# FFN parts of 6, 8 and 8 pairs in place of 8, 7 and 7, with fourteen pairs per FFN as seven block products

## The chip, the cores and the metric

The kernel runs on one core of a Trainium2 chip. The metric is the device time of one execution in microseconds (us), as the median of several; lower is better. All products are made in single precision by splitting each float32 operand into a high and a low part (names that end in hi and lo) and adding three matmuls: high by high, high by low, low by high.

## The reference

A trunk of two layers works on 512 tokens of width 1024 with 16 learned tokens put ahead of them, 528 columns in all. A layer is a mixer (attention, a convolution module and a short convolution side by side) and a feed-forward network (FFN). The change concerns the FFN, and the first step of the next mixer:

```python
def ffn_sublayer(h, pre_g, post_g, w_up, conv_w, w_down):
    u = rms_norm(h, pre_g)
    z = jnp.einsum("bld,df->blf", u, w_up)
    z = causal_depthwise_conv(z, conv_w)
    g, up = jnp.split(z, 2, axis=-1)
    y = jnp.einsum("blf,fd->bld", jax.nn.silu(g) * up, w_down)
    return h + rms_norm(y, post_g)

def reference(x, meta_tokens, ...):
    ...
    for l in range(DEPTH):
        h = mixer_sublayer(h, ...)
        h = ffn_sublayer(h, ...)
    return h[:, N_META:]
```

The hidden width of the FFN is 2816, so w_up makes 2 x 2816 columns: a gate half and an up half.

## The kernel before, in words

**Pairs and parts.** The hidden width is cut into 22 chunks of 128. A *pair* f is the gate chunk and the up chunk with that number. The FFN runs in parts of pairs (PARTS, L29). A part makes the up products of its pairs one after the other, sends each pair through the convolution and the gate (ffn_gate, around L2171 to L2191), which gives one g tile per pair (a high and a low part, the tiles y), and then makes the *down* products of the part: for each of eight output blocks m, the sum over the part's g tiles. Parts 0 and 1 add into the tile yp on the way (L2412: a copy by ScalarE in part 0, a sum by VectorE in part 1); the last part is merged with the normalisation that follows and with the next mixer's first products (finish, L2435). In the last layer the down of parts 0 and 1 is 512 wide and that of the last part is in two halves of 256.

**Whole pairs.** A whole pair is two chunks of 8 blocks of the inner dimension, three matmuls each, in two halves of the columns: 96 matmuls (mm3, L837).

**Pairs as seven block products.** For pairs in SEVEN, seven_pair (L2293) treats the gate and up chunks, and the two halves of the inner dimension, as a 2 x 2 block matrix, and the two column halves of the inputs likewise, and makes seven block products of 12 matmuls in place of eight: 84 matmuls (product, L2288). Its inputs are four sums of blocks of u, the tiles t0 to t3, made once per FFN by normalised (L2212), whose steps are handed out by build between other work. Its weights are the gate chunk itself and three more parts called c, b and d: c and b are read from sums of weight blocks (w_sum in DRAM), d is half of the up chunk. prep_one (L616) loads each part, splits it (ACT casts the high part, L641; DVE subtracts to get the low part, L642), and puts it into tiles: c into the rotating whi and wlo, d into the tile of the largest part's last g, and b into shi and slo, of which there is **one each**.

**The sums of weights** are made ahead, in DRAM, at five kinds of places, which SUMS lists per layer: place 0, in the FFN of the layer before; place 1, in the layer's mixer (L1846: SP copies blocks, and POOL adds with accumulating DMAs; sum_steps, put at L534); place 2, in the FFN by tick (after each g tile one step behind a POOL copy, L2206); places 3 and 4, in the down of parts 0 and 1, by loads to the chip, sums on VectorE and stores (down_sum, L575). Sums are taken in the order of the pairs that need them.

**Stored splits.** While layer 0 runs, six chunks of the next mixer's input weights are split and written to DRAM (w_split), so that the next mixer can load the two parts without splitting. store_one (L663) does one step: it takes the chunk that the call before fetched, casts it into shi on ACT (L666), subtracts into slo on DVE (L667), has POOL write both to DRAM (L670), and fetches the next chunk. It uses the same shi and slo as part b of a seven-product pair. Seven calls do all six: the first only fetches, the last only stores. AHEAD_SPLITS (L2349) lists the pairs of layer 0 ahead of which they stand: two each before pairs 8, 9 and 10 and one before 11.

**What sets the order.** The FFN's up products and the downs of parts 0 and 1 are given in program order and put in order by a scheduler, engine by engine; every engine runs its own instructions strictly in that order and waits on what others have to deliver. issue_after keeps an instruction from standing ahead of a named one on its engine. PE is TensorE, DVE VectorE, ACT ScalarE, POOL GpSimd and SP the engine that issues most loads.

Of the kernel before, what the change touches and what calls it, by code (L numbers as in the profile page):

```python
# [18 lines left out]
KD = D // P  # L19
# [6 lines left out]
CK = 31  # L26
DFF = 2816
NF = DFF // P
PARTS = (8, 7, 7)  # L29


SUMS = (((), (11, 12, 13), (15, 16), (17, 18), (19, 20)),
        ((8, 9), (10, 11, 12, 13), (15, 16), (17, 18), (19, 20)))
SEVEN = tuple(sorted(sum(places, ())) for places in SUMS)
NEXT_SUMS, AHEAD_SPLITS = 13, (8, 8, 9, 9, 10, 10, 11)
SUM_US, SUM_LAT, SUM_EVERY = 0.9, 9.0, 40.0
K2 = KD // 2
SB = K2 * P
AHEAD = 2
# [350 lines left out]
def tile_hybrid_trunk(ctx: ExitStack, tc: tile.TileContext, xT, wflat, pv_d, out):  # L390
# [158 lines left out]
    def sums_at(l, place):  # L549

        return SUMS[l][place] if l < DEPTH else ()

# [572 lines left out]
    def mixer(l, ypool, first, close_first, spans, front, rzs, u_at):  # L1125
# [719 lines left out]

        for i, f in enumerate(sums_at(l, 1)):  # L1846
            copies, *adds = sum_steps(l, f)
            tok = flow.op("sp", 2.0, copies, (Tok(flow.pe + SUM_EVERY * i),), prio=8, lat=SUM_LAT)
            for op in adds:
                tok = gp(SUM_US, op, tok, prio=8, lat=SUM_LAT)  # L1850

# [168 lines left out]
    def y_pair(i):  # L2020
        t = T(ypool, [P, 2, L], F32R, f"y{i}")
        return t[:, 0], t[:, 1]
# [71 lines left out]
    for l in range(DEPTH):  # L2094
# [23 lines left out]
        with tc.tile_pool(name=f"fp{l}", bufs=2, reuse_waits="tile") as fp:  # L2118
# [91 lines left out]
            def normalised():  # L2210
# [39 lines left out]
                        yield lambda b=b, k=k: un(b, k)  # L2250
                for k in range(0, K2, 2):
                    if k:
                        yield None
                        yield lambda: block(0)
                        yield None
                    yield lambda: total(2, k, lambda: at(b12), lambda: at(b22))
                    yield lambda: split(2, k)
                    yield lambda: total(0, k, lambda: at(b11), lambda: at(b12))
                    yield lambda: total(1, k, lambda: at(b22), lambda: raw[0], ALU.add)
                    yield lambda: split(0, k)  # L2260
                    yield lambda: total(3, k, lambda: at(b21), lambda: raw[1])
                    yield lambda: split(1, k)
                    yield lambda: split(3, k)
# [4 lines left out]

            mul_ins, glo_ins, ghi_ins = [None], [None], {}
            ts, n_seven, primed = [], [0], set()  # L2270
            building = [None]

            def build(n):

# [70 lines left out]
            for part, nf in enumerate(PARTS):  # L2345
                for f in range(f0, f0 + nf):
                    if g:
                        tick(g[max(g)][0][:, :1])
                    for _ in range(AHEAD_SPLITS.count(f) if l == 0 else 0):  # L2349
                        store_one()  # L2350
                    if f in seven:
                        seven_pair(f)
                        if f == seven[-1]:
# [29 lines left out]
                if seven and part == 0:  # L2383
                    for k in range(0, KD, 4):
                        nc.sync.dma_start(h_dram[:, k:k + 4], h[:, k:k + 4])
                    spare[0] = h
                if part < len(PARTS) - 1:
                    more = down_sums(l, part)
                    for op in more.pop(-1):
                        op()  # L2390
                    for some in ((0, 1), *((m,) for m in range(2, KD))):
# [12 lines left out]
                        for m, ps in zip(some, tiles):  # L2404
# [8 lines left out]
                            for op in more.pop(m, ()):  # L2413
                                with tc.issue_after(evac.ins), tc.issue_after(last_low[0].ins):
                                    op()
                else:
                    assert not todo and not later and building[0] is None
                    if seven:
# [3 lines left out]
                    gpre = None if final else pvs[l + 1][1][:, _COLS["mix_pre_g"]:]  # L2422
                    first = raw = rzs = None
                    if not final:
                        raw = list(zip(*[g[f0 + k] for k in range(nf)], y_pair(nf)))
                        raw = [[[t[:, half_sl(hf)] for t in ts] for ts in raw] if hf < 2 else None for hf in range(2)]
                        rzs = [rz[:, half_sl(hf)] if raw[hf] else None for hf in range(2)]
                        first = First(lambda b, k, hf, raw=raw: raw[hf][b][k] if raw[hf] else u_rhs(b, k, hf), [H, H], {})
# [62 lines left out]
```

## Time and profile before

| | |
|---|---|
| median of the runs before | 1264.08 us (1263.58 to 1264.17) |
| the profiled execution | 1262.1 us, span of the core 1260.4 us |
| mean granted TensorE clock | 0.999 |
| whole pairs of layer 0's FFN, part 0 | within 276.5 to 411 us |
| seven-product pairs of layer 0, last part | within 518.3 to 568 us |
| seven-product pairs of layer 1, last part | within 1134 to 1183 us |

In the rows of the profile, "psum<-t,whi" names the output and the inputs of an instruction by the program's names; 128x264 is its tile, "x1107" a number of instructions. A bracket "[0.35 <-ACT zs L2373]" means that the engine stood idle for 0.35 us ahead of that instruction, until ACT's instruction on zs at line 2373 let it go. Matmul records overlap, so what one matmul costs is the spacing of the starts, not the printed length. "uhi, ulo" are the split input of a product, "t" the sums of blocks of it. Where a weight is loaded to the tile h or raw, it is the same kind of load into another free place.

### The profile page before, as it was taken

The numbers are of one execution on the slowest core, as the hardware profiler recorded it, in microseconds if no ns is written. First come the engines' busy times: TensorE is split into PE (matmuls) and PEld (weight loads), VectorE is DVE, ScalarE is ACT, GpSimd is POOL, SyncE is SP. The second block draws the span as 40 slices with busy tenths as digits, with TensorE's granted clock in tenths as the row PEclk, the third lists the DMA queues.
The fourth block names the chain that finished last, engine by engine and source line by source line (L and its number), as shares of the span: only waits on it lengthen the run. The fifth ranks groups of instructions, "written<-read, shape, count | busy, mean of one in ns | idle before, by whom it ended". The sixth has DMA issues, their size and how long they took to land.

```text
span 1260.4 us, 24292 instructions
## 1 busy us (share of the span) xinstructions
PE 1244.2 (99%) x9554; PEld 1194.4 (95%) x9554; DVE 926.0 (73%) x1581; ACT 710.3 (56%) x1377; POOL 175.9 (14%) x360
## 2 busy tenths in 40 slices
PE   8999999999999999999999999999999999999997
PEld 8999898999999999999999988999999899989997
DVE  7887866589874776487688877756799748757954
ACT  7254576655444663476673545775554447526763
POOL 1323411001111001010003244110022000000000
PEclk9999999999999999999999999999999999999999
DMA  7267551726658755765652684547166565465611
GB/s 245 80 154 180 122 118 47 256 88 150 185 146 339 243 192 153 243 193 169 209 186 68 157 194 109 144 116 238 70 166 177 148 212 172 151 228 178 203 60 67
DMA packets 80755, 206.59 MB, mean 164 GB/s; under 512 B 8624, under 2 KB 18992, under 8 KB 80128
## 3 DMA queue, kind: packets, MB, share of 16 engines
q1 hardware_dynamic: 66976, 168.20, 42.1%
q0 software_dynamic: 13664, 36.84, 13.0%
q8 instruction: 75, 1.23, 0.4%
q14 instruction: 40, 0.33, 0.1%
HBM read 170.82 MB, written 50.60 MB: 176 GB/s over the span
## 4 chain that ended last, share of the span: by engine, by line
PE 94%; DVE 2%; ACT 1%; DMA 1%; POOL 1%; issue 0%; SPq 0%; DVEq 0%; ACTq 0%
PE psum L837 63%; PE psum L2288 17%; PE psum L1407 5%; PE psum L1671 3%; PE psum L1637 2%; PE psum L974 1%; PE psum L1593 1%; PE psum L1737 1%; PE psum L1323 1%; DMA raw<-in_w_dram 0%; POOL dm L1608 0%; DMA h<-in_x_dram 0%; DVE yp L1050 0%; DVE h L1060 0%; PE psum L1617 0%
## 5 line engine op out<-in xcount | busy, mean ns | idle before, releaser
L837 PE MATMUL psum<-y,whi 128*128 128x264 f32 (+3 forms) x1968 | 383.8, 299 | 0.8 <-DVE zs L989 0.7
L837 PEld LDWEIGHTS psum<-y,whi 128*128 128x128 f32 x1968 | 305.8, 188 | 13.7 <-DVE zs L989 0.9
L837 PE MATMUL psum<-uhi,whi 128*128 128x264 f32 (+1 forms) x1168 | 292.2, 289 | 1.5 <-ACT uhi L2069 0.8
L837 PE MATMUL psum<-ulo,whi 128*128 128x264 f32 (+1 forms) x1168 | 286.0, 284 | 0.6 <-DVE ulo L2071 0.4
L837 PE MATMUL psum<-uhi,wlo 128*128 128x264 f32 (+1 forms) x1168 | 285.3, 284 | 0.0
L837 PE MATMUL psum<-y,wlo 128*128 128x264 f32 (+3 forms) x984 | 274.0, 297 | 0.7 <-DVE wlo L793 0.7
L837 PEld LDWEIGHTS psum<-uhi,whi 128*128 128x128 f32 x1168 | 201.7, 189 | 5.9 <-issue 1.6
L837 PEld LDWEIGHTS psum<-ulo,whi 128*128 128x128 f32 x1168 | 201.8, 189 | 1.3 <-DVE ulo L2071 0.6
L837 PEld LDWEIGHTS psum<-uhi,wlo 128*128 128x128 f32 x1168 | 201.5, 189 | 0.0
L837 PEld LDWEIGHTS psum<-y,wlo 128*128 128x128 f32 x984 | 178.0, 188 | 6.4 <-DVE wlo L793 1.1
L2173 DVE SCALAR_TENSOR_TENSOR c<-zs,pv,c 128x528 f32<-128x528 f32 (+1 forms) x176 | 130.5, 756 | 21.2 <-ACT c L2171 19.9
L652 ACT CAST whi<-raw 128x1024 fp32r<-128x1024 f32 (+1 forms) x65 | 66.1, 1021 | 96.9 <-PE psum L837 74.3
L793 DVE TENSOR_TENSOR wlo<-raw,whi 128x1024 fp32r<-128x1024 f32 (+2 forms) x80 | 95.6, 1204 | 31.1 <-ACT whi L789 30.5
L789 ACT CAST whi<-raw 128x1024 fp32r<-128x1024 f32 (+2 forms) x80 | 81.7, 1030 | 26.3 <-PE psum L837 18.1
L653 DVE TENSOR_TENSOR wlo<-raw,whi 128x1024 fp32r<-128x1024 f32 (+1 forms) x65 | 76.9, 1183 | 20.9 <-ACT whi L652 20.9
L1153 DVE SCALAR_TENSOR_TENSOR cacc<-apad,pv,cacc 128x528 f32<-128x528 f32 x120 | 87.5, 771 | 0.1
L2288 PE MATMUL psum<-uhi,whi 128*128 128x258 f32 (+1 forms) x252 | 71.4, 284 | 0.0
L2288 PE MATMUL psum<-ulo,whi 128*128 128x258 f32 (+1 forms) x252 | 71.3, 283 | 0.0
L2288 PE MATMUL psum<-uhi,wlo 128*128 128x258 f32 (+1 forms) x252 | 70.8, 283 | 0.0
L2171 ACT ACTIVATE c<-zs,pv 128x528 f32<-128x528 f32 (+1 forms) x88 | 63.0, 727 | 6.8 <-DVE zs L2136 2.6
L2206 POOL COPY cols<-y 128x1 f32<-128x1 f32 x24 | 18.4, 767 | 334.7 <-ACT y L2187 334.4
L2288 PE MATMUL psum<-t,shi 128*128 128x258 f32 (+1 forms) x336 | 63.2, 283 | 0.0
(273 smaller groups left out, 2324.4 us busy)
## 6 DMA issues: line engine op xcount, KB each, us to landing
raw<-in_w_dram SPq DMA_DIRECT2D x114, 512.0 KB, 4.6
raw<-in_w_dram SPq DMA_DIRECT2D x30, 448.0 KB, 5.2
h<-in_w_dram SPq DMA_DIRECT2D x25, 512.0 KB, 4.7
raw<-w_sum SPq DMA_DIRECT2D x21, 512.0 KB, 5.2
h<-w_sum SPq DMA_DIRECT2D x21, 512.0 KB, 5.1
h<-in_w_dram POOLq DMA_DIRECT2D x16, 512.0 KB, 4.0
w_sum<-h POOLq DMA_DIRECT2D x16, 512.0 KB, 6.3
w_sum<-in_w_dram SPq DMA_DIRECT2D x26, 256.0 KB, 5.8
```

The source lines that it names most:

```text
L652: nc.scalar.copy(hi[:, :sz], raw[:, :sz])
L653: last_low[0] = nc.vector.tensor_sub(lo[:, :sz], raw[:, :sz], hi[:, :sz].bitcast(F32))
L789: nc.scalar.copy(box["hi"][:, :sz], box["raw"][:, :sz])
L793: nc.vector.tensor_sub(lo[:, :sz], box["raw"][:, :sz], box["hi"][:, :sz].bitcast(F32))
L837: nc.tensor.matmul(d, lhsT=w[a][:, k, cols], rhs=rhs(b, k, hf), start=start and i == 0 and p == 0, stop=stop and i == n - 1 and p == 2)
L1153: nc.vector.scalar_tensor_tensor(conv[j], in0=src, in1=conv[j], scalar=col("a_dw_w", CK * j + i), op0=ALU.mult, op1=ALU.add)
L1407: nc.tensor.matmul(ps[:n, :nw], lhsT=(uhi, ulo)[ui][:, k, P * b:P * b + n], rhs=w[wi][:, k % 4, :], start=k == 0 and p == 0, stop=k == KD ...
L1637: nc.tensor.matmul(s, lhsT=k[:, ka:ka + kn], rhs=q[:, s0:qz], start=i == 0, stop=i == 1)
L1671: nc.tensor.matmul(acc[:, s0 - qa:qz - qa], lhsT=vals[:, b].rearrange("p h d -> p (h d)")[:, o:o + P], rhs=box["p"], start=b == 0, stop=b ...
L2171: nc.scalar.activation(dst, src[:, 2:2 + 2 * fw], AF.Copy, scale=wtap(2, t))
L2173: nc.vector.scalar_tensor_tensor(dst, in0=src[:, i:i + 2 * fw], scalar=wtap(i, t), in1=dst, op0=ALU.mult, op1=ALU.add)
L2288: nc.tensor.matmul(psum[:, bank, :n7], lhsT=w[a][:, k0 + k, :], rhs=rhs(b, k), start=start and k == 0 and p == 0, stop=stop and k == K2 - ...
```

## The change

PARTS becomes (6, 8, 8). More pairs are made as seven products: in layer 0 fourteen (6 to 12 and 14 to 20) in place of nine, in layer 1 fourteen in place of twelve. Pair 13 and the pairs 0 to 5 and 21 stay whole. More sums are made in the mixers (place 1) and by tick (place 2), fewer in the downs (places 3 and 4); the mixer's sums, which were due at steps of 40 us, are now spread evenly over 220 us. The seven calls of store_one no longer stand ahead of pairs 8 to 11, which are now seven-product pairs themselves, but one behind each block or block group of part 1's down in layer 0. normalised no longer gives up its turn ahead of one step once the first down has begun. And as the last part has eight pairs, its eight g tiles (and no spare tile more) take the next mixer's raw input.

```diff
-PARTS = (8, 7, 7)
-SUMS = (((), (11, 12, 13), (15, 16), (17, 18), (19, 20)),
-        ((8, 9), (10, 11, 12, 13), (15, 16), (17, 18), (19, 20)))
+PARTS = (6, 8, 8)
+SUMS = (((), (6, 7, 8, 9, 10, 11, 12, 14), (15, 16, 17), (18,), (19, 20)),
+        ((6, 7), (8, 9, 10, 11, 12, 14), (15, 16, 17), (18,), (19, 20)))
 SEVEN = tuple(sorted(sum(places, ())) for places in SUMS)
-NEXT_SUMS, AHEAD_SPLITS = 13, (8, 8, 9, 9, 10, 10, 11)
-SUM_US, SUM_LAT, SUM_EVERY = 0.9, 9.0, 40.0
+NEXT_SUMS = 13
+SUM_US, SUM_LAT, SUM_SPAN = 0.9, 9.0, 220.0
...
-            tok = flow.op("sp", 2.0, copies, (Tok(flow.pe + SUM_EVERY * i),), prio=8, lat=SUM_LAT)
+            tok = flow.op("sp", 2.0, copies, (Tok(flow.pe + SUM_SPAN * i / len(sums_at(l, 1))),), prio=8, lat=SUM_LAT)
...
                     if k:
-                        yield None
+                        if not downs:
+                            yield None
                         yield lambda: block(0)
...
-            building = [None]
+            building, downs = [None], []
...
-                    for _ in range(AHEAD_SPLITS.count(f) if l == 0 else 0):
-                        store_one()
...
+                downs.append(part)
                 if part < len(PARTS) - 1:
...
                                 with tc.issue_after(evac.ins), tc.issue_after(last_low[0].ins):
                                     op()
+                        if l == 0 and part == 1:
+                            with tc.issue_after(evac.ins), tc.issue_after(last_load[0].ins):
+                                store_one()
...
-                        raw = list(zip(*[g[f0 + k] for k in range(nf)], y_pair(nf)))
+                        raw = list(zip(*[g[f0 + k] for k in range(nf)], *[y_pair(k) for k in range(nf, KD)]))
```

How the instructions move is shown at one place on two engines. First DVE, around the last stores. In the kernel before, this is layer 0 between pairs 10 and 12; slo_5273 is the sixth store (L667), slo_5282 the low part of b of pair 11 (L642), L653 the low parts of whole chunks, and L2173 to L2191 the gate of earlier pairs:

```order
L667 TENSOR_TENSOR slo_5273<-h_2841,shi_5272 128x1024
L653 TENSOR_TENSOR wlo_5065<-h_2841,whi_5064 128x1024
L2173 SCALAR_TENSOR_TENSOR c_5118<-zs_2834,pv_3_69,c_5118 128x528
L2191 TENSOR_TENSOR y_495_4987<-c_4977,y_495_4987 128x528
L2173 SCALAR_TENSOR_TENSOR c_5118<-zs_2834,pv_3_69,c_5118 128x528
L653 TENSOR_TENSOR wlo_5150<-h_2841,whi_5149 128x1024
L2173 SCALAR_TENSOR_TENSOR c_5122<-zs_2834,pv_3_69,c_5122 128x528 x2
L2184 TENSOR_TENSOR c_5118<-c_5118,c_5122 128x528
L2191 TENSOR_TENSOR y_510_5128<-c_5118,y_510_5128 128x528
L642 TENSOR_TENSOR wlo_5206<-raw_5203,whi_5205 128x1024
L642 TENSOR_TENSOR slo_5282<-h_2841,shi_5281 128x1024
```

Between the last store and the b part of the first seven-product pair stand nine rows of other work. In the changed kernel the corresponding rows stand at the end of part 1's down in layer 0; slo_5877 is the third store and slo_6066 the sixth, the two sums of L2412 are those of the last blocks, m = 6 and 7, and the rows of L642 and L653 are weights of the pairs 14 (wlo_6013 is its c, slo_6078 its b, y_617 its d), 15 and 16:

```order
L667 TENSOR_TENSOR slo_5877<-raw_5816,shi_5876 128x1024
L2412 TENSOR_TENSOR yp_2858<-yp_2858,psum_67 128x528 x2
L642 TENSOR_TENSOR wlo_6013<-h_2866,whi_6012 128x1024
L667 TENSOR_TENSOR slo_5940<-raw_5883,shi_5939 128x1024
L653 TENSOR_TENSOR wlo_6115<-h_2866,whi_6114 128x1024
L642 TENSOR_TENSOR y_617_6096<-raw_6094,y_617_6096 128x512
L667 TENSOR_TENSOR slo_6003<-raw_5946,shi_6002 128x1024
L642 TENSOR_TENSOR wlo_6174<-raw_6171,whi_6173 128x1024
L653 TENSOR_TENSOR wlo_6244<-h_2866,whi_6243 128x1024
L667 TENSOR_TENSOR slo_6066<-raw_6009,shi_6065 128x1024
L642 TENSOR_TENSOR slo_6078<-h_2866,shi_6077 128x1024
```

Three stores now stand behind the end of that down, and b of pair 14 directly behind the last of them. On PE, the first product that reads a b tile is, in the kernel before, that of pair 11 (shi_5281; whi_5318 is the first weight of the pair that follows, of which ten of twelve matmuls stand ahead):

```order
L2288 MATMUL psum_67<-uhi_108,whi_5318 128x264
L2288 MATMUL psum_67<-ulo_109,whi_5318 128x264
L2288 MATMUL psum_67<-uhi_108,wlo_5319 128x264
L2288 MATMUL psum_67<-uhi_108,whi_5318 128x264
L2288 MATMUL psum_67<-t_404_3710,shi_5281 128x264 x2
L2288 MATMUL psum_67<-t_404_3710,slo_5282 128x264
```

In the changed kernel, b of pair 14 (shi_6077) follows products of later pairs, the last of them with whi_6173, the c tile of pair 15:

```order
L2289 MATMUL psum_67<-uhi_108,whi_6173 128x264
L2289 MATMUL psum_67<-ulo_109,whi_6173 128x264
L2289 MATMUL psum_67<-uhi_108,wlo_6174 128x264
L2289 MATMUL psum_67<-t_410_3746,shi_6077 128x264 x2
L2289 MATMUL psum_67<-t_410_3746,slo_6078 128x264
L2289 MATMUL psum_67<-t_410_3746,shi_6077 128x264 x2
```

In all, 108 matmuls stand between the last one of part 1's down and this row: 24 each with the tiles whi_5949 (gate of pair 14), whi_6012 (its c), whi_6114 (gate of 15) and whi_6173 (its c), and 12 with whi_6243 (gate of 16). In the kernel before, 34 stand between the last whole pair and the first row that reads shi_5281. Over the whole program PE has 60 matmuls fewer, SP 41 more DMAs and POOL 27 more.

## The prediction

> **What bounds the kernel now.** I read the page's totals first, then its chain of waits, then what TensorE (PE) waited for, and then the stages by windows.
>
> ```profile
> span 1260.4 us, 24292 instructions
> ...
> PE 1244.2 (99%) x9554; PEld 1194.4 (95%) x9554; DVE 926.0 (73%) x1581; ACT 710.3 (56%) x1377; POOL 175.9 (14%) x360
> ...
> PEclk9999999999999999999999999999999999999999
> ...
> PE 94%; DVE 2%; ACT 1%; DMA 1%; POOL 1%; issue 0%; SPq 0%; DVEq 0%; ACTq 0%
> ```
>
> PE is busy for 1244.2 of 1260.4 us at full clock, and 94% of the chain that ended last is PE. The next view gives the columns start, length, what, and how many instructions: the FFN stretches of the chain are PE running into itself, here those of layer 1.
>
> ```profile
> 983.08 39.83 PE psum L837 x171
> ...
> 1134.10 49.28 PE psum L2288 x410
> ...
> 1234.76 11.01 PE psum L837 x93
> ```
>
> So a matmul that is left out of the FFN is worth its whole spacing, and any gap that opens on PE is paid in full: nothing else is there to absorb it. The same in windows (us, then busy time and count of PE, PEld, DVE, ACT and POOL, granted clock, DMA share, GB/s), for layer 0's whole pairs, its seven-product pairs and two stretches of the mixers:
>
> ```profile
> 276.50:411.00 134.50, 134.50 (x1107) 134.50 (x1106) 99.74 (x136) 63.28 (x85) 19.11 (x30) 1.00 0.62 193
> 518.30:568.00 49.70, 49.70 (x411) 49.70 (x411) 37.30 (x48) 35.03 (x61) 4.66 (x5) 1.00 0.68 196
> 20.00:215.00 195.00, 192.58 (x1449) 178.34 (x1449) 151.90 (x345) 111.62 (x280) 55.36 (x124) 1.00 0.49 121
> 660.00:840.00 180.00, 178.12 (x1341) 164.99 (x1342) 139.73 (x323) 102.14 (x261) 58.31 (x123) 1.00 0.54 128
> ```
>
> In the seven-product stretch VectorE (DVE) is busy 37.30 of 49.70 us and ScalarE (ACT) 35.03, so longer runs of such pairs do not make either the bound by their mean load. What counts is the order in which single steps stand.
>
> **Part 1: fewer products.** A whole pair is 96 matmuls, a seven-product pair 84. Spacing in layer 0: 134.50/1107 = 0.1215 us whole, 49.70/411 = 0.1209 us in the seven products. One pair saves 96 × 0.1215 − 84 × 0.1209 = 1.51 us; five more pairs, 7.5 us. In layer 1 the halves of a whole pair are 250 and 264 wide. The wider are as wide as layer 0's, 0.1215 us; a run of 24 of the narrower stands in PE's timeline (start, length) from the first row here to the second:
>
> ```profile
> 881.77 0.28 PE L837 MATMUL psum<-uhi,whi 128*128 128x250 f32 x1
> ...
> 884.46 0.28 PE L837 MATMUL psum<-uhi,wlo 128*128 128x250 f32 x1
> ```
>
> That is 2.69/23 = 0.117 us. A seven-product matmul there is 49.28/410 = 0.120. So 48 × 0.117 + 48 × 0.1215 − 84 × 0.120 = 1.4 us, and two pairs give 2.8. The last layer's down moves one pair from a 512-wide part into the narrow last part: 24 matmuls at 39.83/171 = 0.233 go and 48 at 11.01/93 = 0.118 come, which costs 0.1 us. Together PE's work falls by **10.2 us**. That the change does not make these products is no case: the order lists 84 matmuls for each new pair.
>
> **Part 2: the stores move, and they share tiles with b.** Six chunks of the next mixer's weights are split into the tiles shi and slo, of which there is one each, and written to `w_split` by POOL. Every store must wait until the one before has left slo; so must the b part of the next seven-product pair. Before, this chain ran beside whole pairs. DVE's timeline (start, length, operation, and in brackets the idle time ahead and who ended it):
>
> ```profile
> 399.86 1.23 DVE L667 TENSOR_TENSOR slo<-raw,shi 128x1024 fp32r<-128x1024 f32 x1 [4.25 <-DMA w_split<-slo]
> ...
> 415.54 1.22 DVE L667 TENSOR_TENSOR slo<-raw,shi 128x1024 fp32r<-128x1024 f32 x1 [2.66 <-DMA w_split<-slo]
> ...
> 422.00 1.22 DVE L667 TENSOR_TENSOR slo<-h,shi 128x1024 fp32r<-128x1024 f32 x1
> ...
> 432.78 1.22 DVE L642 TENSOR_TENSOR slo<-h,shi 128x1024 fp32r<-128x1024 f32 x1
> ```
>
> The third to the sixth store are three periods apart in 422.00 − 399.86 us: 7.4 each, and the waits in brackets are for the store before to leave slo. The last row is b of pair 11, done at 434.0; PE first reads it here (shi, then slo two matmuls later):
>
> ```profile
> 439.27 0.41 PE L2288 MATMUL psum<-t,shi 128*128 128x264 f32 x2
> ```
>
> So before, b is 5 us early, and the chain costs nothing. In the changed order (DVE's rows in the section on the change) the fourth to sixth stores stand behind the sums of the last blocks of part 1's down, and b of pair 14 behind them. Call T the moment at which PE ends that down. From T, the fourth slo waits for: twelve matmuls of pair 14 (1.45 us), ACT's negation of them, its cast of c, and DVE's subtraction for c (1.23, as the rows above for tiles of that size). ACT's two, with the length after the start:
>
> ```profile
> 430.56 1.05 ACT L641 CAST whi<-raw 128x1024 fp32r<-128x1024 f32 x1
> ...
> 436.60 0.39 ACT L2314 ACTIVATE psum<-psum 128x264 f32<-128x264 f32 x1
> ```
>
> 1.45 + 0.39 + 1.05 + 1.23 and two short hops make T + 4.3. Three periods of 7.4 later, at T + 26.5, slo can be written for b14, which takes 1.2: T + 27.7. What PE has to do until then is counted from the order: 108 matmuls of pairs 14, 15 and 16, and two on shi before slo is needed, 110 × 0.1209 = 13.3 us. **The stall is 14.4 us.** The cast of c for pair 15 stands behind the sixth store's cast on ACT too, so part of the gap will show at pair 15's c; it ends no later.
>
> Its bounds come from the landing times of the stores:
>
> ```profile
> L670 POOL DMA_DIRECT2D w_split<-slo x6: 531/532/533, 380.9 to 423.5; - x6
> ...
> DMA to landing us min/median/max: 3.0/6.4/8.4
> ```
>
> With every store at 3.0 the period is 1.2 + 3.0 and a 0.4 hop = 4.6 and the stall 4.3 + 3 × 4.6 + 1.2 − 13.3 = 6.0 us; at 8.4 the period is 10.0 and the stall 22. I take the measured periods, since they hold the same casts, queue and tiles. The stores' write time falls by the Trainium skill, "DMA: Bandwidth & Descriptors", in its section on the anatomy of a SWDGE DMA, to 2.0 us + bytes/436e3, an estimate of 3.2 us for 512 KB; by it the stall would be near 6.6 us and the change a gain (rival A). The trace's median of 6.4, with a DMA share of 0.62 there, speaks against it.
>
> **Part 3: what comes with it.** After the stall, b of pair 15 needs the same tiles: its cast (1.05, the row above) can start only when PE has read b14 for the last time. I add 1.1 us (between 0, if PE has other pairs' products, and one period of 7.4, if a store's landing is still in the way; the cast is nearest). The clock may also fall during the gap. The rows for that are the cold start, in PE's timeline,
>
> ```profile
> 1.26 7.87 PE L2034 MATMUL psum<-warm 128*128 128x264 f32 x44 [1.26 <-DVE warm L2032]
> ```
>
> and the last window with PE at work, in which it rests for most of the time and the granted clock is 0.94:
>
> ```profile
> 1252.00:1260.00 8.00, 2.00 (x8) 1.44 (x8) 4.14 (x8) 1.17 (x2) 0.00 (x0) 0.94 0.39 131
> ```
>
> Forty-four matmuls take 7.87 us where 44 × 0.1209 would be 5.3: a cold start costs up to 2.5 us. I take half, 1.3 us, bounds 0 and 2.5, as the gap may be broken in two by pair 15's c. The Trainium skill, "TensorE: Matmul & The Clock Gate", says in Part 1 on the HAM clock gate that one idle window of about 3.4 us halves the clock and about as long a busy one restores it: a rule against any change that opens such a gap, with which these rows agree.
>
> Last, nine more pairs' sums go through POOL's accumulating DMAs (two come out of the down stages, seven are new), most of them in the mixers: 27 more. The nearest rows are such sums now, by the tile's shortest, median and longest time (ns), then what POOL and PE wait for there (us, times, longest):
>
> ```profile
> L534 POOL DMA_DIRECT2D w_sum<-w_sum x26: 796/844/890, 66.2 to 984.7; - x26
> ```
>
> ```profile
> POOL w_sum L534 <- DMA w_sum<-in_w_dram: 20.3, 4, 6.6
> ```
>
> ```profile
> PE psum L1617 <- POOL dm L1608: 1.4, 2, 1.0
> ```
>
> POOL is busy 55.36 of 195 us in the first mixer stretch, so 15 more DMAs of 0.8 us there fit; PE has waited for POOL's dm only 1.4 us. But POOL is in order, and a DMA that waits 6.6 us for its source holds dm back. Bounds: −1 (if the earlier sums ease the down stages) and +3; I take 0.5, near to PE's present waits. Raw u in the g tiles and SP's 41 more issues lie beside PE's work: nothing.
>
> **The sum.** −10.2 + 14.4 + 1.1 + 1.3 + 0.5 = +7.1 us. The profiled execution took 1262.1 (span 1260.4 and 1.7 around it), 2 us under the median; so 1269.2 there and, carried to the median of 1264.1, **1271**.
>
> **The rivals.**
>
> A, *the stores land fast enough*: period 4.6, stall 6.0 and follow-ups 1 to 2: −10.2 + 7.5 = −2.7, 1261; or the chain is covered by something that I read too late, down to the full gain, 1254. For: the minimum landing of 3.0; and while PE stands, few new weights can be loaded, which thins the traffic. Against: the median landing of 6.4 and the periods of 7.4, which are the same steps. The Trainium skill's page on DMA, above, would give this case. Break-even is a stall near 8, a period of 5.2. Chance 0.24.
>
> B, *the stall takes just the gain*: period about 5.5, stall 8.7 and 1 to 2 more: 1262 to 1266. Chance 0.08.
>
> C, *POOL's queue becomes late in the mixers*, on the slow side: if each of the two mixers loses one longest wait of 6.6 us in front of dm, 13 us come on top, at least 8: 1279 to 1284. It decides once a DMA's wait on its source exceeds the slack of dm. Against: POOL's load of 28 to 32% there. Chance 0.08.
>
> The forecast, a stall of 10 to 22 us in layer 0 and a slower kernel between 1266.7 and 1279, keeps 0.60.
>
> **How the numbers follow.** About 0.2%, 2.5 us, is what a measurement of this kernel can tell from no change. Faster 0.24 (A), same 0.08 (B), slower 0.68 (forecast and C). The range runs from 1257, the middle of A's faster half, to 1279, where C begins: it leaves out about 0.1 of A and 0.08 of C. The forecast's own range is 1267 to 1279.
>
> **What would show it.** Right: in the changed profile 60 matmuls fewer; in PE's waits one or two rows on L2289 of some 14 us for ACT's shi or DVE's slo, 10 to 28 us after part 1's down in layer 0; DVE waits for the landing of `w_split`; granted clock under 1.00 in that window; no other new PE wait over 1 us. Wrong: no gap behind part 1's down, stores that land in 3 us, or gaps of that size in the mixers or in layer 1, where no stores run.

## The result, and the profile after

The changed kernel takes 1306.1 us (median of four, 1304.19 to 1314.92) against 1264.1 before, 42 us slower; the ratio of the runs' means is 1.0346, with an interval of 1.0305 to 1.0386. (The ratios below are of means too.) The prediction had the sign right and the size wrong: it said 1271, in a range of 1257 to 1279. The execution that was profiled took 1314.9 us, 9 us above the median, with a span of 1313.2. The terms below are measured in that one execution (52.8 us of span more than before); the experiments, which are timed, give the same terms for medians.

From the page of the changed kernel:

```profile
span 1313.2 us, 24363 instructions
...
PE 1259.9 (96%) x9494; PEld 1204.4 (92%) x9494; DVE 935.1 (71%) x1589; ACT 729.5 (56%) x1421; POOL 207.0 (16%) x387
...
PEclk9998999999989999799999999999999899999999
...
PE 74%; DMA 10%; DVE 7%; issue 5%; ACT 3%; POOL 1%; SPq 1%; DVEq 0%; ACTq 0%; POOLq 0%
```

PE has 60 matmuls fewer, as counted, and yet is 15.7 us longer "busy": it has run part of them on a slow clock (the line PEclk now has dips). PE's share of the chain fell from 94% to 74%, and 10% of it are now transfers. What PE waited for (us in all, times, longest):

```profile
PE psum L837 <- ACT whi L652: 10.6, 2, 5.9
PE psum L2289 <- ACT whi L641: 8.9, 3, 4.2
PE psum L1593 <- DMA k<-pair_lo: 5.3, 1, 5.3
PE psum L974 <- DVE acc L934: 3.4, 3, 2.6
PE psum L837 <- DVE zs L989: 2.0, 1, 2.0
```

These rows lie at five places: the first is split over the downs of part 0 in both layers, the second is the start of pair 14 in layer 0, the third and the fourth are layer 0's mixer, the fifth is the start of layer 1's mixer. The same by windows (us; busy time and count of PE, PEld, DVE, ACT, POOL; granted clock; DMA share; GB/s):

```profile
515.00:555.00 40.00, 28.11 (x164) 25.51 (x163) 15.79 (x17) 15.01 (x22) 2.66 (x5) 0.81 0.71 249
360.00:380.00 20.00, 15.34 (x108) 15.13 (x108) 12.97 (x18) 8.79 (x13) 0.56 (x1) 0.83 0.67 214
1018.00:1038.00 20.00, 12.81 (x44) 9.57 (x43) 11.74 (x15) 8.02 (x12) 0.57 (x1) 0.83 0.63 217
```

Counts tell the loss better than idle time, since they also hold the slow clock. At 0.1209 us a matmul 40 us hold 331: pair 14's start lost 167 × 0.1209 = 20.2 us. Part 0's down of layer 0 made 108 of 165 and lost 7 us; that of layer 1 (512 wide, 0.233 us each) 44 of 86 and lost 10. The mixers have no such window, as PE's work there is uneven; so I take the first g tile of layer 0's FFN, ACT's first cast of line 2187. Before, and then in the changed kernel:

```profile
290.94 0.63 ACT L2187 CAST y<-c 128x528 fp32r<-128x528 f32 x1 [1.27 <-DVE c L2184]
```

```profile
309.36 0.64 ACT L2187 CAST y<-c 128x528 fp32r<-128x528 f32 x1
```

18.4 us have gone before the FFN's first g tile, ahead of the first pair that the change makes another way. From layer 0's last such cast to layer 1's first it is 325.4 us before (596.5 to 921.9) and 337.4 after (628.7 to 966.1); 5.8 of that are the 48 matmuls of the eighth pair in the last part's down, so 6 us are lost there. The account is −10.2 + 20.2 + 18.4 + 7 + 10 + 6 = 51.4 of the 52.8 us.

### The profile page after: what moved, and what is told of

Same layout as the page of the kernel before. It is cut to its first block, busy times and chain, and to the rows that moved or that the text cites. A ratio compares the mean times of both kernels' runs of the same rounds, so it can differ in the third digit from the quotient of the medians.

```text
span 1313.2 us, 24363 instructions
## 1 busy us (share of the span) xinstructions
PE 1259.9 (96%) x9494; PEld 1204.4 (92%) x9494; DVE 935.1 (71%) x1589; ACT 729.5 (56%) x1421; POOL 207.0 (16%) x387
## 4 chain that ended last, share of the span: by engine, by line
PE 74%; DMA 10%; DVE 7%; issue 5%; ACT 3%; POOL 1%; SPq 1%; DVEq 0%; ACTq 0%; POOLq 0%
PE psum L837 41%; PE psum L2289 19%; PE psum L1407 4%; DMA raw<-in_w_dram 4%; PE psum L1671 3%; PE psum L1637 2%; DMA w_sum<-in_w_dram 2%; PE psum L974 2%; DMA w_sum<-h 1%; DVE wlo L793 1%; DMA h<-in_w_dram 1%; ACT whi L789 1%; PE psum L1593 1%; DVE c L2173 1%; PE psum L1737 1%
## 5 line engine op out<-in xcount | busy, mean ns | idle before, releaser
L837 PE MATMUL psum<-uhi,whi 128*128 128x264 f32 (+1 forms) x944 | 247.5, 291 | 2.3 <-ACT uhi L1066 0.9
L837 PE MATMUL psum<-ulo,whi 128*128 128x264 f32 (+1 forms) x944 | 241.9, 285 | 0.9 <-DVE ulo L1068 0.5
L837 PE MATMUL psum<-uhi,wlo 128*128 128x264 f32 (+1 forms) x944 | 241.8, 285 | 0.0
L837 PEld LDWEIGHTS psum<-uhi,whi 128*128 128x128 f32 x944 | 168.0, 190 | 7.2 <-issue 2.0
L837 PEld LDWEIGHTS psum<-ulo,whi 128*128 128x128 f32 x944 | 168.2, 190 | 1.8 <-DVE ulo L1068 0.9
L837 PEld LDWEIGHTS psum<-uhi,wlo 128*128 128x128 f32 x944 | 168.2, 190 | 0.0
L2173 DVE SCALAR_TENSOR_TENSOR c<-zs,pv,c 128x528 f32<-128x528 f32 (+1 forms) x176 | 130.5, 756 | 20.0 <-ACT c L2171 18.6
L793 DVE TENSOR_TENSOR wlo<-raw,whi 128x1024 fp32r<-128x1024 f32 (+1 forms) x80 | 97.2, 1224 | 43.1 <-ACT whi L789 42.6
L789 ACT CAST whi<-raw 128x1024 fp32r<-128x1024 f32 (+1 forms) x80 | 83.1, 1046 | 41.8 <-DMA raw<-in_w_dram 21.5
L2289 PE MATMUL psum<-uhi,whi 128*128 128x264 f32 (+1 forms) x336 | 97.0, 289 | 1.7 <-ACT psum L2315 0.9
L652 ACT CAST whi<-raw 128x1024 fp32r<-128x1024 f32 (+1 forms) x54 | 53.4, 993 | 78.9 <-PE psum L837 48.0
L2289 PE MATMUL psum<-ulo,whi 128*128 128x264 f32 (+1 forms) x336 | 96.0, 286 | 0.0
L2289 PE MATMUL psum<-uhi,wlo 128*128 128x264 f32 (+1 forms) x336 | 94.4, 285 | 0.0
L2289 PE MATMUL psum<-t,shi 128*128 128x264 f32 (+1 forms) x448 | 84.7, 284 | 0.9 <-ACT zs L2323 0.5
L653 DVE TENSOR_TENSOR wlo<-raw,whi 128x1024 fp32r<-128x1024 f32 (+1 forms) x54 | 62.2, 1151 | 12.8 <-ACT whi L652 11.4
L2289 PEld LDWEIGHTS psum<-t,shi 128*128 128x128 f32 x448 | 69.3, 189 | 1.3 <-ACT zs L2323 0.7
```

Source lines behind the costliest of these rows:

```text
L652: nc.scalar.copy(hi[:, :sz], raw[:, :sz])
L653: last_low[0] = nc.vector.tensor_sub(lo[:, :sz], raw[:, :sz], hi[:, :sz].bitcast(F32))
L789: nc.scalar.copy(box["hi"][:, :sz], box["raw"][:, :sz])
L793: nc.vector.tensor_sub(lo[:, :sz], box["raw"][:, :sz], box["hi"][:, :sz].bitcast(F32))
L837: nc.tensor.matmul(d, lhsT=w[a][:, k, cols], rhs=rhs(b, k, hf), start=start and i == 0 and p == 0, stop=stop and i == n - 1 and p == 2)
L2173: nc.vector.scalar_tensor_tensor(dst, in0=src[:, i:i + 2 * fw], scalar=wtap(i, t), in1=dst, op0=ALU.mult, op1=ALU.add)
```

## The experiments

The theory after the two traces: three edits cost separately, namely (1) the store chain at pair 14, (2) the additional sums in layer 0's mixer, (3) the sum made in the down of part 0, which is now only six pairs long. Against it stood that the parts of 6, 8 and 8 are bad by themselves, or that one overload of transfers makes all gaps together. Every time below is a median beside runs of the kernel before on the same chip (1262.6 to 1263.7 us).

**Extra sums alone, in the kernel before.** The sums of seven more pairs are made and read by nobody. As in the change, all sums of a mixer are spread over 220 us in place of steps of 40 us, so the sums that were there already move to later times too:

```diff
+EXTRA = ((6, 7, 8, 9, 10), (6, 7))
...
-        for i, f in enumerate(sums_at(l, 1)):
+        made = (*EXTRA[l], *sums_at(l, 1))
+        for i, f in enumerate(made):
             copies, *adds = sum_steps(l, f)
-            tok = flow.op("sp", 2.0, copies, (Tok(flow.pe + SUM_EVERY * i),), prio=8, lat=SUM_LAT)
+            tok = flow.op("sp", 2.0, copies, (Tok(flow.pe + SUM_SPAN * i / len(made)),), prio=8, lat=SUM_LAT)
```

> The kernel before, with seven more pairs' weight sums made in the mixers (five in layer 0, two in layer 1, spread over 220 us as in the changed kernel) and read by nobody. Theory, queues: the extra sums stand in the in-order queues of SP and POOL and hold back the mixers' own copies and masks; in the two traces layer 0's first g tile came 18.5 us later and layer 1's mixer cost 6 us more, so this kernel should take 1280 to 1290 us. Rival, that these delays come from the changed FFN or from one bad execution: 1264 to 1267 us.

Measured: 1278.4 against 1263.3, ratio 1.0118 (1.0102 to 1.0135): 15 us. The matmuls of this kernel are those of before, so the start of the k-th one can be compared, from the traces (us; the three further columns belong to the experiments below):

```
k-th PE instruction   before   sums: later by   copies alone   adds alone   stores in down
  650 (attention)       88.0        0.2            -0.2           5.6            1.4
  806                  109.7        4.4             0.4           7.7            1.5
 1700                  231.8        5.9             0.4           8.0            1.5
 1828 (mixer's end)    247.6       13.0             6.8          13.3            1.5
 2300 (FFN)            306.5       16.2             9.4          17.7            1.5
 3900                  501.8       16.2             9.4          17.6            1.0
 4300 (last part)      550.3       16.2             9.8          17.6           22.7
 9500 (end)           1243.5       17.7            14.3          17.8           24.5
```

So the sums cost at two places of layer 0's mixer: 6 us by instruction 1700, most of it where PE waits for the heads' k (806), and 10 at the mixer's end. In layer 1 the two extra sums cost 1.5 us in this run (4.5 with the copies alone, below).

**Copies alone, and adds alone.** Of the seven extra sums either only SP's copies or only POOL's adds are made.

```diff
-            for op in adds:
+            for op in adds if f in sums_at(l, 1) else ():
```

> As the first experiment (the kernel before with seven more pairs' sums in the mixers), but of the seven extra sums only SP's copies are made, no adds by POOL. That whole experiment cost 15 us. Theory P, POOL's queue: POOL waited 121 us for the copies of sums in place of 20, and its masks stand behind these waits; without the adds nothing is lost: 1263 to 1266 us. Theory S, SP's queue: three copies stand ahead of the heads' own copies on SP: 1273 to 1279 us. Theory D, the DMA engines are shared and the traffic itself slows all transfers: about half, 1267 to 1272 us.

```diff
-            copies, *adds = sum_steps(l, f)
+            copies, *adds = sum_steps(l, f, scratch[l] if i and f in EXTRA[l] else None)
...
+            if i == 0 or f in sums_at(l, 1):
                 tok = flow.op("sp", 2.0, copies, (tok,), prio=8, lat=SUM_LAT)
```

> As the one before, the other half: of the seven extra sums only POOL's 21 accumulating adds are made, all into the first extra sum's space of each layer, which alone is copied by SP; the values are read by nobody. Theory P, POOL's queue: 1272 to 1279 us, or more, since each add waits for the one before. Theory S, SP's queue: 1263 to 1266 us. Theory D, shared DMA engines: 1267 to 1272 us.

Measured: copies alone 1273.7 (ratio 1.0078, 1.0061 to 1.0095), 11 us; adds alone 1281.8 (1.0148, 1.0133 to 1.0163), 19 us. By theory P the first, by theory S the second should have cost nothing; theory D said "about half" each, and both cost more than that. The halves together, 30 us, are twice the whole. The table shows why: from instruction 1700 to 2300, at the mixer's end, the three runs lose 10.3, 9.0 and 9.7 us, so each half pays there nearly what both pay. But there the halves are not clean. The old sums have moved in all three runs: with the copies alone, POOL's nine adds, all of old sums, stand between 199 and 272 us, and in the kernel before between 58 and 162. So the two times do not tell the queues apart at the mixer's end. Theory P's own wait is not seen there, though: with the copies alone PE waited 0.8 us in all for POOL's dm, and 5.6 us at once for acc, which the loads at the mixer's end feed. What is lost there shows on SP's queue (start, length, how many): the reload of h, in the kernel before, in the changed one, with the copies alone and with the adds alone:

```profile
217.92 3.45 SPq L494 DMA_DIRECT2D h<-in_x_dram  x7
```

```profile
225.10 5.44 SPq L494 DMA_DIRECT2D h<-in_x_dram  x7
```

```profile
218.35 7.79 SPq L495 DMA_DIRECT2D h<-in_x_dram  x7
```

```profile
225.91 8.82 SPq L495 DMA_DIRECT2D h<-in_x_dram  x7
```

Seven issues take 5 to 9 us in place of 3.45, and the weight load behind them is late. In the chain of the changed kernel the mixer's end is a row of loads with their cast and subtraction between them:

```profile
230.63 9.76 DMA raw<-in_w_dram
...
242.75 5.78 DMA raw<-in_w_dram
```

In the window 205 to 250 us the DMA share rises from 0.57 before to 0.82 after (0.73 with the copies alone, 0.79 with the adds alone):

```profile
205.00:250.00 45.00, 45.00 (x354) 43.28 (x353) 22.22 (x33) 28.57 (x57) 1.25 (x8) 1.00 0.57 189
```

```profile
205.00:250.00 45.00, 45.00 (x357) 43.41 (x356) 21.58 (x38) 26.58 (x58) 9.33 (x17) 1.00 0.82 202
```

PE itself stands still only after that stretch, so the window that shows the cause looks healthy on PE. In the attention, where the copies alone, with no add yet made, cost nothing (0.4 us at instruction 806) and the adds alone 7.7, the adds are needed for the loss; whether by POOL's order or by their traffic was not separated. POOL's waits for the sums' own transfers are, in the changed kernel:

```profile
POOL w_sum L534 <- DMA w_sum<-in_w_dram: 133.3, 17, 20.4
```

**The stores elsewhere.** In the changed kernel, the calls of store_one stand ahead of whole pairs of part 0 (AHEAD_SPLITS is (2, 3, 3, 4, 4, 5, 5)):

```diff
+                    for _ in range(AHEAD_SPLITS.count(f) if l == 0 else 0):
+                        store_one()
...
-                        if l == 0 and part == 1:
-                            with tc.issue_after(evac.ins), tc.issue_after(last_load[0].ins):
-                                store_one()
```

> The changed kernel, with the seven calls of store_one ahead of the whole pairs 2 to 5 of layer 0 in place of part 1's down. Theory, store chain: the stretch around pair 14's start, where PE made 163 matmuls in 40 us in place of 331 (20 us lost), closes; 1306 - 20 = 1286 us (1283 to 1290). Rival, that weight loads behind the DMA traffic make that gap and the stores only lie there: 1300 us or more.

Measured: 1298.6 (ratio 1.0271, 1.0251 to 1.0291); expected were 1283 to 1290. The gap at pair 14 is closed, as this window of its start shows, with 332 matmuls in 40 us:

```profile
500.00:540.00 40.00, 40.00 (x332) 40.00 (x331) 19.52 (x23) 13.48 (x19) 2.32 (x3) 1.00 0.77 240
```

Instruction for instruction against the changed kernel it wins 21 us around pair 14 (from the 3846th to the 4300th), but it had lost 11 by then, between the 2190th and the 2600th, where the stores now stand: beside the whole pairs of part 0 the stores cost as well.

**The stores' place alone, in the kernel before.** The seven calls move behind the blocks of part 1's down and AHEAD_SPLITS goes; nothing else is edited.

> The kernel before with one edit of the change alone: the seven calls of store_one behind the blocks of part 1's down in layer 0. Theory, store chain: the b part of pair 15 waits for the last stores, and the kernel loses what the changed one loses there, 15 to 21 us: 1279 to 1285 us. Rival, that the chain hurts only together with the longer run of seven-product pairs or the heavier traffic: 1264 to 1270 us.

Measured: 1285.5 (ratio 1.0178, 1.0163 to 1.0193): 22 us for this edit alone. The last column of the table above has the place: 1.0 us late at instruction 3900, 22.7 at 4300, which lies in the last part, some 32 us behind its start.

**Other tiles for the stores.** The same place as in the changed kernel, but the rotating weight tiles in place of shi and slo:

```diff
-            hi, lo = (T(tx[0], [P, 2 * SB], F32R, t) for t in ("shi", "slo")) if sz <= 2 * SB else (...)
+            hi, lo = (T(tx[0], [P, 2 * SB], F32R, t) for t in ("shi", "slo")) if False else (...)
```

> The changed kernel with the stores at the same place, but cast and subtracted into the rotating weight tiles whi and wlo in place of shi and slo. Theory, shared tiles: b of pair 14 no longer waits for the stores, and the stall of 20 us goes, 1286 us, less what held weight tiles cost, up to 1298 us. Rival, late stores delay DVE and ACT whatever tiles they use: 1302 to 1310 us.

Measured: 1293.5 (ratio 1.0249, 1.023 to 1.0268), within what the theory of shared tiles allowed; against the changed kernel it wins 17 us between the 3846th and the 4300th instruction, and loses 7 between the 3600th and the 3846th, in the down, where the stores now hold weight tiles.

**Does POOL's queue delay the chain?** The pairs 19 and 20 of layer 0 whole, so that part 1's down makes no sums there:

```diff
-SUMS = (((), (6, 7, 8, 9, 10, 11, 12, 14), (15, 16, 17), (18,), (19, 20)),
+SUMS = (((), (6, 7, 8, 9, 10, 11, 12, 14), (15, 16, 17), (18,), ()),
```

> The changed kernel with the pairs 19 and 20 of layer 0 whole (24 matmuls more, 3 us), so that no sums of weights are made in the down of part 1 there. In the changed kernel the first store's slo left only at 489 us, 25 us after its shi, since POOL's queue held the down sums' stores ahead of it. Theory Q, POOL's queue delays the start of the store chain: it now ends 20 us earlier and the stall of 20 us at pair 14 all but goes: 1289 to 1294 us. Rival, the chain is late because each store stands behind its own block's sum on DVE: 1306 to 1310 us.

Measured: 1300.9 (ratio 1.0302, 1.0275 to 1.0329), between the two expectations. The theory falls: the first slo is still subtracted only at 481.94 us,

```profile
481.31 0.70 DVE L2412 TENSOR_TENSOR yp<-yp,psum 128x528 f32<-128x528 f32 x1 [2.85 <-PE psum L837]
481.94 1.22 DVE L667 TENSOR_TENSOR slo<-raw,shi 128x1024 fp32r<-128x1024 f32 x1
```

directly behind a block's sum on DVE, as the rival had it. Six stores at some 7 us each do not fit behind blocks of which the last ends part 1. The 4 us that it won against the changed kernel (38 in place of 42 over the kernel before; 7 with the 3 for the two whole pairs) I have not taken apart.

**No sum in part 0's down.** Pair 18 whole in both layers:

```diff
-SUMS = (((), (6, 7, 8, 9, 10, 11, 12, 14), (15, 16, 17), (18,), (19, 20)),
-        ((6, 7), (8, 9, 10, 11, 12, 14), (15, 16, 17), (18,), (19, 20)))
+SUMS = (((), (6, 7, 8, 9, 10, 11, 12, 14), (15, 16, 17), (), (19, 20)),
+        ((6, 7), (8, 9, 10, 11, 12, 14), (15, 16, 17), (), (19, 20)))
```

> The changed kernel with pair 18 whole in both layers, so that no sum of weights is made in the down of part 0 (24 matmuls more, 3 us). Theory, held slots: weight loads of that down wait in SP's queue until a finished sum has left the spare places of h; PE's gaps there with the slow clock after them cost 7 us in layer 0 and 11 in layer 1, and go: 1306 - 18 + 3 = 1291 us (1288 to 1296). Rival, that a down of only six pairs is too short for its weight loads in any case: 1309 us.

Measured: 1292.3 (ratio 1.0232, 1.0214 to 1.0251), as expected. The window that held the gap of layer 0 is full (167 matmuls in 20 us):

```profile
355.00:375.00 20.00, 20.00 (x167) 20.00 (x167) 13.80 (x17) 12.62 (x18) 0.00 (x0) 1.00 0.50 138
```

How the gap arises stands in the changed kernel's queues, first SP's around it, then what SP waited for:

```profile
360.13 0.34 SPq L650 DMA_DIRECT2D raw<-in_w_dram  x1
368.30 1.55 SPq L650 DMA_DIRECT2D h<-in_w_dram  x2
```

```profile
SPq L650 <- DMA w_sum<-h: 20.0, 6, 7.8
```

The weight loads at 368.30 go to the places of h that the sum occupied, and start when its store has landed (POOL issued it at 358.13; it landed at 368.25). PE, out of weights, restarts at 374.60. The kernel before has two sums in this down, but over eight pairs, a third longer.

**Back towards the kernel before.** Three kernels with parts of 6, 8 and 8 take the costly moves back in part. The ninth has nine seven-product pairs in layer 0, three sums in its mixer and the stores at the old place, with three sums in part 1's down:

```diff
+SUMS = (((), (11, 12, 14), (15, 16, 17), (), (18, 19, 20)),
+        ((6, 7), (8, 9, 10, 11, 12, 14), (15, 16, 17, 18), (), (19, 20)))
+NEXT_SUMS, AHEAD_SPLITS = 13, (8, 8, 9, 9, 10, 10, 11)
```

> The changed kernel with its three costly moves taken back: layer 0 keeps nine seven-product pairs (11, 12, 14 to 20) with three sums in its mixer, the stores stand ahead of the whole pairs 8 to 11 again, and no sum is made in the down of part 0 (three in that of part 1 in layer 0). Layer 1 keeps its fourteen. Theory, three separate costs: what is left is layer 1's gain of 2.8 us, so 1260 to 1262 us, unless the third sum in part 1's down holds weight loads back (then up to 1268). Rival, the parts of 6, 8 and 8 cost something by themselves: 1266 us or more.

The tenth has (9, 10, 11, 12, 14) in layer 0's mixer and AHEAD_SPLITS (6, 6, 7, 7, 8, 8, 8); the eleventh (10, 11, 12, 14), tick makes (15, 16, 17, 18), layer 1's mixer makes seven, and AHEAD_SPLITS is (7, 7, 8, 8, 9, 9, 9).

> As the ninth, with eleven seven-product pairs in layer 0 (9 to 12 and 14 to 20), five sums in its mixer and the stores ahead of pairs 6 to 8. Theory, a mixer can carry some more sums as long as none runs when h is loaded back near 220 us: two more pairs save 3 us, 1257 to 1260 us. Rival, every sum beyond three costs the mixer as the extra seven did (2 us each): 1263 to 1267 us.

> As the ninth, with ten seven-product pairs in layer 0 (10 to 12 and 14 to 20), four sums in its mixer, pair 18's sum of layer 0 made by tick instead of in part 1's down, and in layer 1 seven sums in the mixer. Stores ahead of pairs 7 to 9. Theory: one pair more saves 1.5 us and the down of part 1 is lighter: 1258 to 1261 us. Rival, sums beyond three cost the mixer 2 us each: 1261 to 1264 us, and layer 1's mixer, with seven, loses too: up to 1268.

All three missed: 1275.8 (ratio 1.0109, 1.0083 to 1.0135), 1275.4 (1.0108, 1.0084 to 1.0131) and 1282.2 (1.0154, 1.0139 to 1.0169). Each had a gap at another place of the same kind. The ninth stood 4.1 us at pair 14 and 3.1 at pair 11; on SP, loads for seven-product pairs waited 33.5 us, once 17.2, for stored sums to leave their places (19.9 and 6.8 in the kernel before):

```profile
SPq L631 <- DMA w_sum<-h: 33.5, 5, 17.2
```

The tenth stood 4.0 us at pair 14 and 2.8 in part 0's down. The eleventh stood in both mixers (PE waited 11.9 us for POOL's masks, five times). It is not the number of sums alone that decides. With five of them in layer 0's mixer, the tenth casts its first g tile at 292.0 us, only 1.1 later than the kernel before; its seven issues of h took 3.45 us, and none of POOL's adds was issued between 213 and 235 us. With four, the eleventh casts it at 307.3. So in layer 0's mixer the tenth's theory holds, sums that do not meet the reload of h fit, and its rival of 2 us for each sum falls; the tenth lost its time elsewhere. Nor does a late sum alone cost much: the ninth and the twelfth (next), with three sums and their last adds at 211 to 228 us, are 0.3 and 0.4 us late there. The last kernel relieves the two places of the ninth:

```diff
+SUMS = (((), (11, 12, 14), (15, 16, 17, 18), (), (19, 20)),
+        ((6,), (8, 9, 10, 11, 12, 14), (15, 16, 17, 18), (), (19, 20)))
+NEXT_SUMS, AHEAD_SPLITS = 13, (7, 7, 8, 8, 9, 9, 9)
```

> As the ninth, with the two places where it still stood relieved: pair 18's sum of layer 0 made by tick, so that part 1's down makes two sums in place of three, and the stores ahead of pairs 7 to 9, so that a whole pair (10) lies between the last of them and the first seven-product pair (11). Layer 1 makes thirteen pairs (6, 8 to 12, 14 to 20). Theory, each gap has its own neighbour: no gap of over 2 us is left in layer 0's FFN, and the time is that of before less 1.4 us for one more pair, plus 1 to 3 us at the start of layer 1's mixer: 1262 to 1266 us. Rival, the parts of 6, 8 and 8 cost by themselves, about 10 us as in the ninth: 1270 us or more.

Measured: 1267.5 against 1263.7 (ratio 1.0029, 1.0017 to 1.004), above the 1262 to 1266 that were expected. The FFN of layer 0 has no gap over 0.6 us left, so the parts do not cost 10 us by themselves. But 3.8 us and the 1.4 of the pair saved are still lost. In the profiles 2 of them lie between layer 0's last g tile and layer 1's first, beyond the 5.8 of the eighth pair, and 2 behind that. Whether the parts by themselves cost these was not tested. PE's longest waits are now

```profile
PE psum L837 <- DVE zs L989: 2.0, 1, 2.0
PE psum L1081 <- DVE yp L1050: 1.4, 1, 1.4
...
PE psum L837 <- ACT yp L2412: 1.1, 1, 1.1
PE psum L1671 <- POOL p L1651: 1.0, 1, 1.0
```

of which the first (0.7 us before, 2.0 in every kernel above with eight pairs in the last part) is the start of layer 1's mixer. No version that beats the kernel before was found.

## Why the prediction was right in sign and wrong in size

**Fewer products: right.** 9494 matmuls for 9554. The 10 us were not timed alone; the account above closes with them. So does the sum of the timed experiments: 15.1 (sums) + 22.2 (stores) + 16 (the sum in part 0's down: 13 between the two kernels' differences to before, and 3 for the whole pairs) − 10.2 = 43 us, and the change measured 42. The two small edits, of normalised's turn and of the last part's raw tiles, were not run alone; that sum leaves little for them.

**The store chain: right in place and mechanism, a little short.** The prediction misread the traffic in the kernel before: the DMA share of 0.62 is that of all whole pairs of part 0, and while the six stores ran there, from 380 to 424 us, it was 0.87. DVE in the changed kernel, from the last block's sum at 516.5 to b of pair 14:

```profile
516.52 0.70 DVE L2412 TENSOR_TENSOR yp<-yp,psum 128x528 f32<-128x528 f32 x1 [5.12 <-PE psum L837]
...
524.25 1.22 DVE L667 TENSOR_TENSOR slo<-raw,shi 128x1024 fp32r<-128x1024 f32 x1
...
531.59 1.22 DVE L667 TENSOR_TENSOR slo<-raw,shi 128x1024 fp32r<-128x1024 f32 x1
...
540.02 1.22 DVE L667 TENSOR_TENSOR slo<-raw,shi 128x1024 fp32r<-128x1024 f32 x1
...
544.52 1.22 DVE L642 TENSOR_TENSOR slo<-h,shi 128x1024 fp32r<-128x1024 f32 x1 [3.27 <-issue]
```

With T at 516.3, where pair 14's first product starts, b is done at T + 29.4; predicted was T + 27.7. The periods were 6.8 us in the mean against 7.4, and they are the stores' landings, as predicted: in the trace the stores of the fourth, fifth and sixth slo land at 531.31, 539.85 and 544.44 us, and the next subtraction into slo starts 0.28, 0.17 and 0.08 us later. The start was later, T + 7.9 and not T + 4.3, since c of pair 14 had not landed when ACT came to it. PE's rows are not those that the prediction named, though, one or two of some 14 us for shi or slo:

```profile
523.12 0.81 PE L2289 MATMUL psum<-t,whi 128*128 128x264 f32 x2 [2.97 <-ACT whi L641]
...
537.76 0.81 PE L2289 MATMUL psum<-t,whi 128*128 128x264 f32 x2 [4.17 <-ACT whi L641]
...
545.80 0.39 PE L2289 MATMUL psum<-t,slo 128*128 128x264 f32 x1 [0.42 <-DVE slo L642]
```

PE stood first for c of pairs 14 and 15, whose loads landed late, and crept on at half the clock behind both gaps; so when it came to b's slo it had only 0.4 us left to wait. The late c of pair 14 also moved the start of the chain. An earlier c of pair 15 would not have helped: by these times the sixth slo could not be written before 539.85, when the fifth had landed. The loss with what follows it was 20.2 against 14.4 + 1.1 + 1.3 = 16.8 us. Rival A, with stores that land in 3 us, falls: they took 2.9 to 9.4, median 6.9. With it falls the estimate of 3.2 us from the Trainium skill's page "DMA: Bandwidth & Descriptors".

**The sums: the step that failed.** "So 15 more DMAs of 0.8 us there fit", at 0.5 us with a bound of +3, measured 15 us in the run with the extra sums alone. Two things were wrong in it. I read POOL's mean load and PE's present waits, which say nothing of how little slack the transfers had; and I looked only at POOL's masks, while most of the loss is at the mixer's end, where the rows to read were the DMA share around the reload of h, with the later times that the new spacing gives the sums, and the chain of load, cast and subtraction of w_out behind it. Rival C had the sums in the mixers as one cause of a slower kernel, 8 to 13 us on top of the stall, but through POOL alone, at 0.08.

**Part 0's shorter down: not in the sum at all.** The change was costed by pairs. That the down of part 0 shrinks from 8 × 48 to 8 × 36 matmuls, while a sum made in it still holds places of h until its store has landed, has no term in the sum; the only word on the downs was a bound of −1, should the earlier sums ease them. It cost 16 us, both layers together. The gaps of 5.3 us in layer 0's mixer and 5.9 in layer 1's down are also what the prediction had listed as signs of being wrong. The sign was not luck: −10.2 + 20.2 us, as measured for the two large terms that it had, already make a slower kernel.

**The clock: right, but paid at every gap.** The prediction added one cold restart. In the changed kernel the granted clock falls at each of the longer gaps. PE's windows (us, busy and count, granted clock, DMA share, GB/s) around the gap in part 0's down:

```profile
370.00:374.60 4.60, 0.00 (x0) 0.78 0.50 173
374.60:378.10 3.50, 3.50 (x16) 0.50 0.26 66
378.10:385.00 6.90, 6.90 (x54) 0.90 0.46 161
```

After 4.6 us without a matmul sixteen of them take 3.5 us, 0.22 each in place of 0.12, and at 0.90 over the next 6.9 us the half clock lasts some 5 us in all. Shorter gaps did it too. These are the windows behind PE's gaps of 3.0 us (pair 14) and 2.6 us (the end of layer 0's mixer):

```profile
523.10:526.50 3.40, 3.24 (x13) 0.50 0.34 88
257.20:259.50 2.30, 2.30 (x6) 0.50 1.06 313
```

By the rule of the Trainium skill that the prediction quoted, "TensorE: Matmul & The Clock Gate", Part 1, it takes one idle window of about 3.4 us, and then about as long a busy one. The gap of 4.6 us fits it; the gaps of 3.0 and 2.6 us are shorter than its words allow, and the measurement decides: here they halved the clock as well.

## What to carry to other kernels

A change that saves work on a saturated engine must be costed by what it asks of the queues that feed it, stage by stage: each extra transfer needs a place in time where nobody's load stands behind it, and a mean share of a queue does not show such a place. When a stage gets shorter, list everything that was hidden in it and what it holds until it is done. Where several small delays are possible, look for each separately: here three edits cost 15, 22 and 16 us, and removing any one alone would have shown a slower kernel still.

## What the runs showed of the hardware that I had not expected

Issuing itself slows when the DMA engines are loaded. SP's seven loads of h took 3.45 us at a DMA share of 0.68 in that stretch (kernel before), 4.65 at 0.72 (the twelfth), 7.8 at 0.93 (copies alone) and 8.8 at 0.90 (adds alone); in the changed kernel they took 5.4 at 1.04, so the share alone does not set the time. A 512 KB weight load behind them took 9.8 us in the changed kernel, where the median of such loads is 4.6 in the kernel before. And the losses of two halves of a traffic do not add up to that of the whole: 11 us for the copies, 19 for the adds (in that run written to one place, each behind the one before), 15 for both, each of the three with the old sums moved as well.
